# Raw tokens transposed at once, with the norm's weight folded into the low-rank weights

## The chip, the cores and the metric

The kernel runs on one core of a Trainium2 chip. A core has TensorE (PE, which multiplies 128x128 stationary tiles with moving ones into PSUM), VectorE (DVE), ScalarE (ACT), GpSimd (POOL) and SyncE (SP, which here only issues DMAs). The metric is the device time of one execution in microseconds, as the median of several.

## The reference

One decoder layer on x of 512 tokens by 1024 channels, all in float32. What matters here is its start:

```python
h = rms_norm(x, norm_g[l])      # x * rsqrt(mean(x*x) + EPS) * norm_g
proj = h @ w_in[l]
hq, hf, hi, hz, cq, ckv, kr, mz, glog = jnp.split(proj, pts, axis=-1)
y_a = hgrn2_branch(hq, hf, hi, hz, lower_bounds[l], hg_norm_g[l])
y_b = mla_branch(cq, ckv, kr, mz, q_a_g[l], w_uq[l], kv_a_g[l], w_ukv[l])
```

The low-rank columns cq, ckv and kr (384, 256 and 64 wide, 704 together) go through a norm or a rotation of their own. All other columns of proj read the same h. A gated recurrence (y_a), attention (y_b), gates, two projections, the output product and a last norm follow.

## The kernel before

Products are made in three parts: each operand is split into a high part (fp32r) and a low part (the rest), and `mm3` (L99) issues high x high, high x low and low x high into one PSUM bank. The high part is a ScalarE copy, the low part a VectorE subtraction (`load_w`, L110, for weights). The split, transposed input h is `hT`, two tiles of 128 x 8 x 512 (channels of a block k, blocks, tokens).

The first stage (L292 to L347) is written out by hand for PE, ACT and DVE: inside `manual_schedule` each engine runs what the code issues, in that order. Behind it a scheduler chooses the order. Tokens are in four tiles of 128 (t = 0 to 3), channels in eight blocks (k). The stage does, per token tile:

- the root: `squares` (L256) sums the squares on ScalarE and makes the power -0.5 on GpSimd (`power`, L174); tile 0 has its own version with a square root on ScalarE and seven small VectorE instructions (L307 to L317);
- `scaled` (L261): VectorE multiplies x by the root and by norm_g, which four matmuls have spread over the partitions into the two banks `ng` (L302 to L304);
- `turned` (L266): TensorE transposes eight 128x128 blocks, ScalarE copies them as the high part and VectorE subtracts for the low part;
- `c_product` (L277): the first 256 low-rank columns, 24 matmuls a tile, into two banks `c_ps`, with weights split by `c_hi` and `c_lo`.

`idle_mm` (L244) issues matmuls on zeros as filler. Then two banks are copied to `c_sb` (L393), and the second low-rank product makes the other 448 columns (L395 to L400): four tiles of tokens by eight blocks by three parts, 96 matmuls, with four weight pieces of two blocks each (`load_c2`, L287). The first two pieces are split inside the first stage, the other two behind it. PSUM has three `mm` banks: two hold the first product, so the second product's tile 1 waits until the first of them is copied out. The small work on the recurrence's lower bound (`lbw`, L376 to L390) lies between. Behind the 96 matmuls come the recurrence's projections, which read hT and split weights of their own (L129, L130), and the norm, transposes and splits of the low-rank columns (L401 to L429). DMAs are issued by SP in the order of the code; a weight buffer's next load waits for VectorE's low part of the last one.

Of the kernel before, what the change touches and what calls it, by code (L numbers as in the profile page):

```python
# [38 lines left out]
def hybrid_layer(ctx: ExitStack, tc: tile.TileContext, a):  # L39
# [158 lines left out]
    ng_row = st.tile([2, 512], F32, "ng_row")
    ng_r = [st.tile([P, 512], F32R, f"ng_r{i}") for i in range(2)]
    zf = st.tile([P, 512], F32, "zf")  # L200
    nc.gpsimd.memset(zf[:], 0.0)
    nc.gpsimd.memset(pick[:], 0.0)
    nc.gpsimd.memset(pick[0:2, 1], 1.0)
    nc.gpsimd.memset(pick[0:1, 1], 0.0)
    nc.gpsimd.memset(pick[0:1, 0], 1.0)
# [43 lines left out]
    def c_hi(kh, i, eng):  # L249
        eng(c_hl[kh][0][:, half[i]], c_raw[kh][:, half[i]])  # L250

    def c_lo(kh, i, eng):
        hi, lo = c_hl[kh]
        eng.tensor_tensor(lo[:, half[i]], c_raw[kh][:, half[i]], hi[:, half[i]].bitcast(F32), op=ALU.subtract)

    def squares(t):  # L256
        sq = st.tile([P, D], F32, "sq", bufs=2)
        nc.scalar.activation(sq[:], x_sb[t][:], AF.Square, accum_out=rss[t][:, 0:1])
        power(rss[t][:, 0:1], rss[t][:, 0:1], 1.0 / D, EPS, neg_half[:, 0:1])

    def scaled(t):  # L261
        for n in range(2):
            nc.vector.scalar_tensor_tensor(xns[t][:, half[n]], x_sb[t][:, half[n]], rss[t][:, 0:1], ng[n][:],
                                           op0=ALU.mult, op1=ALU.mult)

    def turned(t, k4):  # L266

        ps = ax_tile()
        for k in range(4):
            kk = 4 * k4 + k  # L270
            nc.tensor.transpose(ps[:, k * P : k * P + P], xns[t][:, kk * P : kk * P + P], ident[:])
# [1 line left out]
        nc.scalar.copy(hT[0][sl], ps[:].rearrange("p (k t) -> p k t", k=4))
        return lambda: nc.vector.tensor_tensor(hT[1][sl], ps[:].rearrange("p (k t) -> p k t", k=4),
                                               hT[0][sl].bitcast(F32), op=ALU.subtract)

    def c_product(t, kh, kind, ks=range(4)):  # L277

        l, r = ((0, 0), (0, 1), (1, 0))[kind]
        ps = c_ps[t // 2][:, t % 2 * 256 : t % 2 * 256 + 256]  # L280
        for k in ks:
            nc.tensor.matmul(ps, hT[l][:, 4 * kh + k, t * P : t * P + P], c_hl[kh][r][:, k * 256 : k * 256 + 256],  # L282
                             start=kh == 0 and kind == 0 and k == 0, stop=kh == 1 and kind == FIN and k == 3)
# [1024 lines left out]
```

## Time and profile before

| | us |
|---|---|
| median of 3 runs (606.27 to 607.28) | 607.03 |
| the profiled execution | 606.53 |
| its span on the core | 604.7 |
| granted TensorE clock, mean | 0.996 |
| TensorE busy | 595.2 |
| VectorE / ScalarE / GpSimd busy | 445.2 / 283.0 / 148.3 |

The profiled execution's own time is 1.8 above its span. A row of the order in time reads: start, length, engine, line, operation, what it writes and reads, shape, count; in brackets the engine's idle time before it and what ended that. PE rows are matmuls; they are pipelined, so a row's length is longer than the distance to the next. Line numbers are those of the kernel before unless said otherwise.

### The profile page before, as it was taken

What the parts mean: (1) busy time and instruction counts of PE and PEld (TensorE: products, weight loads), DVE (VectorE), ACT (ScalarE), POOL (GpSimd) and SP (SyncE); (2) the same over time, 40 slices, a digit from 0 to 9 for tenths busy, and PEclk for the clock granted to TensorE, in tenths of its full rate; (3) what the DMA queues carried; (4) which work ended last, traced back from release to release, by engine and by line L of the source; (5) the groups of instructions that cost most, each with busy time, mean ns of one, the idle gap of its engine ahead of it and who ended that gap; (6) DMA issues with size and microseconds to landing.
All of it is one profiled execution on the core that took longest, in us unless ns stands there. A gap on an engine that the chain in (4) does not pass through costs nothing.

```text
span 604.7 us, 8828 instructions
## 1 busy us (share of the span) xinstructions
PE 595.2 (98%) x3198; PEld 501.5 (83%) x3198; DVE 445.2 (74%) x689; ACT 283.0 (47%) x517; POOL 148.3 (25%) x253
## 2 busy tenths in 40 slices
PE   9999999999999999999999999999999999999994
PEld 6998888888888888888888888888888888888883
DVE  7717989599764548959767776778878878466795
ACT  7555245333313342436545554456557764153553
POOL 3107322254350237415245540400000000000003
PEclk9999999999999999999999999999999999999998
DMA  8449479997969967582369676888666656366313
GB/s 281 159 137 345 155 220 370 318 223 169 239 152 253 232 194 155 112 186 76 62 153 175 147 159 154 222 289 244 192 187 204 204 182 188 123 233 257 102 36 139
DMA packets 73036, 115.34 MB, mean 191 GB/s; under 512 B 7561, under 2 KB 37663, under 8 KB 72993
## 3 DMA queue, kind: packets, MB, share of 16 engines
q1 hardware_dynamic: 63740, 90.99, 47.2%
q0 software_dynamic: 8336, 22.55, 20.2%
q10 hardware_dynamic: 916, 1.25, 0.6%
q8 instruction: 25, 0.41, 0.3%
q14 instruction: 19, 0.15, 0.1%
HBM read 106.38 MB, written 39.85 MB: 242 GB/s over the span
## 4 chain that ended last, share of the span: by engine, by line
PE 89%; DVE 4%; DMA 3%; ACT 2%; issue 1%; POOL 1%; SPq 0%; POOLq 0%; ACTq 0%; DVEq 0%
PE mm_ps L102 19%; PE mm_ps L104 19%; PE mm_ps L103 19%; PE ax_ps L889 16%; PE mm_ps L889 3%; PE ax_ps L754 1%; PE ax_ps L728 1%; DMA x<-x 1%; PE mm_ps L282 1%; PE ax_ps L556 1%; DVE ya L1173 1%; PE ax_ps L558 1%; PE ax_ps L518 1%; PE ax_ps L104 1%; PE ax_ps L103 1%
## 5 line engine op out<-in xcount | busy, mean ns | idle before, releaser
L130 DVE TENSOR_TENSOR w_lo<-w_raw,w_hi 128x1024 fp32r<-128x1024 f32 (+3 forms) x116 | 138.9, 1204 | 68.9 <-ACT w_hi L129 66.1
L129 ACT CAST w_hi<-w_raw 128x1024 fp32r<-128x1024 f32 (+3 forms) x116 | 114.8, 1007 | 132.6 <-PE mm_ps L103 54.7
L102 PE MATMUL mm_ps<-hT,w_hi 128*128 128x512 f32 x256 | 101.0, 395 | 0.0
L103 PE MATMUL mm_ps<-hT,w_hi 128*128 128x512 f32 x256 | 100.3, 392 | 0.0
L104 PE MATMUL mm_ps<-hT,w_lo 128*128 128x512 f32 x256 | 100.2, 393 | 0.0
L102 PE MATMUL mm_ps<-w_hi,hT 128*128 128x512 f32 (+1 forms) x160 | 61.7, 390 | 0.0
L103 PE MATMUL mm_ps<-w_lo,hT 128*128 128x512 f32 (+1 forms) x160 | 61.5, 385 | 0.0
L104 PE MATMUL mm_ps<-w_hi,hT 128*128 128x512 f32 (+1 forms) x160 | 61.4, 385 | 0.0
L104 PEld LDWEIGHTS mm_ps<-hT,w_lo 128*128 128x128 f32 x256 | 48.1, 188 | 9.9
L102 PEld LDWEIGHTS mm_ps<-hT,w_hi 128*128 128x128 f32 x256 | 48.1, 188 | 9.5
L103 PEld LDWEIGHTS mm_ps<-hT,w_hi 128*128 128x128 f32 x256 | 48.1, 188 | 9.4
L889 PE MATMUL ax_ps<-w_hi,s 128*128 128x512 f32 x208 | 51.5, 389 | 0.0
L889 PEld LDWEIGHTS ax_ps<-w_hi,s 128*128 128x128 f32 x208 | 39.0, 188 | 8.1
L1190 POOL TENSOR_SCALAR ssum<-ssum 128x1 f32<-128x1 f32 x3 | 0.7, 225 | 163.7 <-ACT z L1177 163.6
L104 PEld LDWEIGHTS mm_ps<-w_hi,hT 128*128 128x128 f32 x160 | 30.1, 188 | 5.5
L102 PEld LDWEIGHTS mm_ps<-w_hi,hT 128*128 128x128 f32 x160 | 30.0, 188 | 5.2
L103 PEld LDWEIGHTS mm_ps<-w_lo,hT 128*128 128x128 f32 x160 | 30.1, 188 | 5.1
L736 ACT ACTIVATE p<-ax_ps,sm 128x128 f32<-128x128 f32 (+3 forms) x32 | 16.8, 526 | 35.6 <-DVE sm L735 35.4
L738 POOL TENSOR_SCALAR p<-p,sm 128x128 f32<-128x128 f32 (+3 forms) x28 | 15.6, 563 | 65.0 <-DVE sm L737 54.3
L889 PE MATMUL ax_ps<-w_lo,s 128*128 128x512 f32 x104 | 27.8, 389 | 0.0
L466 DVE RECIPROCAL tf<-pr 128x512 f32<-128x512 f32 x8 | 26.8, 3348 | 0.1
L889 PEld LDWEIGHTS ax_ps<-w_lo,s 128*128 128x128 f32 x104 | 19.5, 188 | 4.0
(319 smaller groups left out, 1189.1 us busy)
## 6 DMA issues: line engine op xcount, KB each, us to landing
w_raw<-w_in SPq DMA_DIRECT2D x54, 512.0 KB, 7.0
g_t<-w_in SPq DMA_DIRECT2D x16, 512.0 KB, 8.9
w_raw<-g_t SPq DMA_DIRECT2D x16, 512.0 KB, 4.7
g_t<-w_in POOLq DMA_DIRECT2D x8, 512.0 KB, 10.5
pa_t<-w_proj_a SPq DMA_DIRECT2D x8, 512.0 KB, 8.4
g_t<-g_t POOLq DMA_DIRECT2D x8, 512.0 KB, 10.0
out_t<-w_out SPq DMA_DIRECT2D x8, 512.0 KB, 9.6
s<-h POOLq DMA_DIRECT2D x8, 512.0 KB, 11.7
```

Of the source, the lines that this page charges most:

```text
L102: nc.tensor.matmul(ps, lh[lsl], rh[rsl], start=start, stop=False)
L103: nc.tensor.matmul(ps, lh[lsl], rl[rsl], start=False, stop=False)
L104: nc.tensor.matmul(ps, ll[lsl], rh[rsl], start=False, stop=stop)
L129: last_hi[0] = nc.scalar.copy(hi[:, :o], raw[:, :o])
L130: last_lo[0] = nc.vector.tensor_tensor(lo[:, :o], raw[:, :o], hi[:, :o].bitcast(F32), op=ALU.subtract)
L282: nc.tensor.matmul(ps, hT[l][:, 4 * kh + k, t * P : t * P + P], c_hl[kh][r][:, k * 256 : k * 256 + 256], start=kh == 0 and kind == 0 and k ...
L466: nc.vector.reciprocal(rp[:], pr[:])
L518: nc.tensor.matmul(sps[:, sl], kt_[:, sl], v_sb[i][:, (h % 4) * P : (h % 4) * P + P], start=True, stop=True)
L556: nc.tensor.matmul(ops[:, sl], asb[:, sl], v_sb[i][:, (h % 4) * P : (h % 4) * P + P], start=True, stop=i == 0)
L736: last_act[0] = nc.scalar.activation(p[:, :n], sps[:, :n], AF.Exp, scale=SCALE, bias=sm[:, 1:2], accum_out=sm[:, 2:3])
L738: scaled_p = (nc.vector if final else nc.gpsimd).tensor_scalar(p[:, :n], p[:, :n], sm[:, 3:4], 0.5, op0=ALU.mult, op1=ALU.mult)
L889: nc.tensor.matmul(ps[:, o : o + n], ap[i][:, k, t * P : t * P + P], w[k // 2][j][:, k % 2, o : o + n], start=fresh and c == 0, stop=c == ...
```

## The change

- x is transposed as it is loaded, before any norm: `turned` reads `x_sb` and fills `xT`, a new pair like hT. A third copy, plain, goes to `ya` (the recurrence's later output buffer, allocated earlier).
- norm_g is loaded as eight rows, transposed once into the column tile `gcol`, and multiplied into the low-rank weights as they are split: `times_g` makes the high part on ScalarE with a scale, and the low part on VectorE with one three-operand instruction, a block at a time (256 or 448 wide).
- The tokens' roots `rs` (all four by `squares`, which now needs no special version) are applied where the low-rank banks are copied to `c_sb`, as a scale of the ScalarE copy.
- h itself is made later: VectorE makes four diagonal tiles of roots, four matmuls with ones spread them over the partitions (`scales`), VectorE multiplies ya by norm_g and the roots (eight instructions of 128x512), and ScalarE and VectorE split the result into hT (eight each).
- ident and the norm's rows are loaded from ScalarE's queue, ident no longer from SP's. The warm-up activation is Tanh, not Sqrt.

```diff
     load_x(0, 2)
-    nc.scalar.dma_start(ng_row[:], a["norm_g"].rearrange("l (n c) -> (l n) c", n=2))
-    nc.sync.dma_start(ident[:], a["c_ident"])
+    nc.scalar.dma_start(ident[:], a["c_ident"])
+    nc.scalar.dma_start(g_rows[:], a["norm_g"].rearrange("l (k p) -> (l k) p", p=P))
...
+    def times_g(hi, lo, src, k0, n, width):
+
+        for k in range(n):
+            sl, g = slice(k * width, k * width + width), gcol[:, k0 + k : k0 + k + 1]
+            nc.scalar.activation(hi[:, sl], src[:, sl], AF.Copy, scale=g)
+            nc.vector.scalar_tensor_tensor(lo[:, sl], src[:, sl], g, hi[:, sl].bitcast(F32), op0=ALU.mult, op1=ALU.subtract)
...
-            nc.tensor.transpose(ps[:, k * P : k * P + P], xns[t][:, kk * P : kk * P + P], ident[:])
+            nc.tensor.transpose(ps[:, k * P : k * P + P], x_sb[t][:, kk * P : kk * P + P], ident[:])
...
+        nc.scalar.copy(xT[0][sl], v)
+        nc.vector.tensor_tensor(xT[1][sl], v, xT[0][sl].bitcast(F32), op=ALU.subtract)
+        return lambda: nc.scalar.copy(ya[sl], v)
...
     with tc.manual_schedule(engines={mybir.EngineType.PE, mybir.EngineType.Activation, mybir.EngineType.DVE}):
         nc.vector.memset(zero[:], 0.0)
+        nc.scalar.activation(warm[:], eps, AF.Tanh)
+        idle_mm(5)
+        plain = [turned(0, 0), turned(0, 1)]
+        ps = ax_tile()
+        nc.tensor.transpose(ps[:, :KD], g_rows[:], ident[:KD, :KD])
+        nc.vector.tensor_copy(gcol[:], ps[:, :KD])
+        for f in plain:
+            f()
+        idle_mm(6)
+        c_split(0)
+        c_product(0, 0, 0)
+        c_product(0, 0, 2)
+        plain = [turned(1, 0), turned(1, 1)]
+        c_product(0, 0, 1)
+        c_split(1)
+        c_products(1, 0)
+        c_products(0, 1)
...
+        c_products(2, 0)
+        plain = [turned(3, 0), turned(3, 1)]
+        c_products(2, 1)
+        c_second = [load_c2(j) for j in range(2)]
+        for f in plain:
+            f()
         for t in range(1, NT):
+            squares(t)
+        c_products(3, 0)
+        c_products(3, 1)
...
-    for t2, ps in enumerate(c_ps):
-        nc.scalar.copy(c_sb[:, 2 * t2 : 2 * t2 + 2, 0:256], ps[:].rearrange("p (t c) -> p t c", t=2))
+    for t in range(NT):
+        nc.scalar.activation(c_sb[:, t, 0:256], c_ps[t // 2][:, t % 2 * 256 : t % 2 * 256 + 256], AF.Copy, scale=rs[:, t : t + 1])
     c_second += [load_c2(j) for j in range(2, 4)]
+    scales = ax_tile()
+    for t in range(NT):
+        nc.vector.tensor_scalar(diag[t][:], ident[:], rs[:, t : t + 1], None, op0=ALU.mult)
+        nc.tensor.matmul(scales[:, t * P : t * P + P], ones[:], diag[t][:], start=True, stop=True)
+    for k in range(KD):
+        nc.vector.scalar_tensor_tensor(ya[:, k], ya[:, k], gcol[:, k : k + 1], scales[:], op0=ALU.mult, op1=ALU.mult)
+        split(hT[0][:, k], hT[1][:, k], ya[:, k])
```

The next pieces show the order that each engine now runs; line numbers in them are each kernel's own. First TensorE inside the second low-rank product, before: mm_ps_438, 464 and 490 are the banks of token tiles 0, 1 and 2, w_hi_427 and w_lo_428 the third weight piece (blocks k 4 and 5). 29 of the 96 matmuls stand ahead of the first row on w_hi_427, 35 ahead of the first on w_lo_428.

```order
L102 MATMUL mm_ps_490<-w_hi_361,hT0_125 128x448
L103 MATMUL mm_ps_490<-w_lo_362,hT0_125 128x448
L102 MATMUL mm_ps_438<-w_hi_427,hT0_125 128x448
L102 MATMUL mm_ps_464<-w_hi_427,hT0_125 128x448
L104 MATMUL mm_ps_490<-w_hi_361,hT1_126 128x448
L102 MATMUL mm_ps_490<-w_hi_367,hT0_125 128x448
L103 MATMUL mm_ps_490<-w_lo_368,hT0_125 128x448
L104 MATMUL mm_ps_490<-w_hi_367,hT1_126 128x448
L103 MATMUL mm_ps_438<-w_lo_428,hT0_125 128x448
```

The same place in the changed kernel: mm_ps_462 and 488 are the banks of tiles 0 and 1, w_hi_414 and w_lo_415 the third weight piece, and diag0 to diag3 the four tiles of roots. Twelve matmuls of tile 0 (k 0 to 3) stand ahead of these rows.

```order
L370 MATMUL ax_ps_429<-diag0_104,ones_103 128x128
L370 MATMUL ax_ps_429<-diag1_105,ones_103 128x128
L102 MATMUL mm_ps_488<-w_hi_328,xT0_126 128x448
L103 MATMUL mm_ps_488<-w_lo_329,xT0_126 128x448
L104 MATMUL mm_ps_488<-w_hi_328,xT1_127 128x448
L102 MATMUL mm_ps_488<-w_hi_328,xT0_126 128x448
L370 MATMUL ax_ps_429<-diag2_106,ones_103 128x128
L370 MATMUL ax_ps_429<-diag3_107,ones_103 128x128
L103 MATMUL mm_ps_488<-w_lo_329,xT0_126 128x448
L104 MATMUL mm_ps_488<-w_hi_328,xT1_127 128x448
L102 MATMUL mm_ps_462<-w_hi_414,xT0_126 128x448
L102 MATMUL mm_ps_488<-w_hi_336,xT0_126 128x448
```

The next row is the first on w_lo_415. So the third weight piece is now read behind 18 of the 96 matmuls (its low part behind 20), not 29 (35), and the four matmuls on the roots stand ahead of it.

ScalarE from tile 3's high parts on, before: hT is the high part, w_hi 128x896 a weight piece of the second product, c_sb the copies of the banks.

```order
L273 CAST hT_125<-ax_ps 128x4x128 x4
L129 CAST w_hi<-w_raw 128x896 x2
L393 COPY c_sb<-mm_ps 128x2x256 x2
L129 CAST w_hi<-w_raw 128x896
L379 ACT_TABLE_LOAD
L379 ACTIVATE lbw<-lbw 128x16
L129 CAST w_hi<-w_raw 128x896
L400 COPY c_sb<-mm_ps 128x448
```

And in the changed kernel, from the same place: the third and fourth weight pieces are the second group of w_hi.

```order
L264 CAST xT_126<-ax_ps 128x4x128 x2
L248 ACTIVATE w_hi<-w_raw,gcol 128x448 x4
L266 COPY ya<-ax_ps 128x4x128 x2
L253 ACTIVATE sq,rs<-x 128x1024 x3
L365 ACTIVATE c_sb<-mm_ps,rs 128x256 x4
L351 ACTIVATE lbw<-lbw 128x16
L248 ACTIVATE w_hi<-w_raw,gcol 128x448 x4
L171 CAST hT_128<-ya 128x512 x4
```

The two plain copies and the squares of three token tiles now stand between the first two weight pieces and the copies of the banks; a table load is gone.

VectorE behind the first stage in the changed kernel: diag_107 is diag3, and w_lo 128x448 x4 are the low parts of the third and fourth piece.

```order
L369 TENSOR_SCALAR diag_107<-ident,rs 128x128
L340 TENSOR_SCALAR hg_half<-par 128x1
L348 TENSOR_TENSOR lbw<-par 128x8
L349 TENSOR_TENSOR lbw<-par,lbw 128x8
L350 TENSOR_TENSOR lbw<-par,lbw 128x8
L352 TENSOR_TENSOR lbw<-lbw 128x8
L353 RECIPROCAL lbw<-lbw 128x8
L355 TENSOR_TENSOR lb<-lbw 128x8
L360 TENSOR_SCALAR c_403<-lb 128x8
L361 TENSOR_SCALAR c1n<-lb 128x8
L362 TENSOR_SCALAR c_405<-lb 128x8
L249 SCALAR_TENSOR_TENSOR w_lo<-w_raw,gcol,w_hi 128x448 x4
```

Before, the third piece's low part stood ahead of the second half of lbw; now all of lbw, and diag3 ahead of it, come first. L352 waits for ScalarE's exponential (L351). Behind these rows stand the eight multiplications of ya, the eight low parts of hT, and then the recurrence's first weights.

More of the change, by code (lines that the diff above doesn't have):

```diff
@@ L186, in hybrid_layer @@
     maskf = cw.tile([P, 2, P], F32, "maskf")
+    rs = cw.tile([P, NT], F32, "rs")
+    gcol = cw.tile([P, KD], F32, "gcol")
+    ones = cw.tile([P, P], F32, "ones")
+    diag = [cw.tile([P, P], F32, f"diag{t}") for t in range(NT)]
     st = Pool("start", "right")
+    raw_pool = Pool("raw_tokens", "left")
     ident = const.tile([P, P], F32, name="ident")
@@ L192, in hybrid_layer @@
     nc.gpsimd.memset(neg_half, -0.5)
+    nc.gpsimd.memset(ones[:], 1.0)
     zero = st.tile([P, 512], BF16, "zero")
-    pick = st.tile([P, 2, P], F32, "pick")
-    pick_r = st.tile([P, 2, P], F32R, "pick_r")
     warm = st.tile([P, 1], F32, "warm")
[L198 to L205, printed above, removed]
+    g_rows = st.tile([KD, P], F32, "g_rows")
     x_sb = [st.tile([P, D], F32, "x", bufs=NT) for _ in range(NT)]
+    xT = [raw_pool.tile([P, KD, S], F32R, f"xT{i}") for i in range(2)]
     hT = [hpool.tile([P, KD, S], F32R, f"hT{i}") for i in range(2)]
+    ya = ypool.tile([P, H, S], F32, tag="ya", name="ya")
     w_c0 = w_in[:, COL_C : COL_C + 256].rearrange("(k p) c -> p k c", p=P)
@@ L247, in idle_mm @@
             nc.tensor.matmul(idle[:], zero[:, :P], zero[:], start=True, stop=True)
[L249 to L254, printed above, removed]
-    def squares(t):
[L257 to L264, printed above, removed]
+    def times_g(hi, lo, src, k0, n, width):
[3 more added lines that the diff above has]
+            nc.vector.scalar_tensor_tensor(lo[:, sl], src[:, sl], g, hi[:, sl].bitcast(F32), op0=ALU.mult, op1=ALU.subtract)
+    def squares(t):
+        sq = st.tile([P, D], F32, "sq")
+        nc.scalar.activation(sq[:], x_sb[t][:], AF.Square, accum_out=rs[:, t : t + 1])
+        power(rs[:, t : t + 1], rs[:, t : t + 1], 1.0 / D, EPS, neg_half[:, 0:1])
     def turned(t, k4):
@@ L302, in hybrid_layer @@
-        for x in range(2):
-            for n in range(2):
-                nc.tensor.matmul(ng[n][:], pick_r[:, n], ng_r[x][:], start=x == 0, stop=x == 1)
-            idle_mm(2 + 2 * x)
-        sq, rs = st.tile([P, D], F32, "sq", bufs=2), rss[0]
-        v, y, e = [st.tile([P, 1], F32, f"rsq{i}") for i in range(3)]
-        for n in range(2):
-            nc.scalar.activation(sq[:, half[n]], x_sb[0][:, half[n]], AF.Square, accum_out=rs[:, n : n + 1])
-        nc.vector.tensor_scalar(v[:], rs[:, 0:1], 1.0 / D, EPS, op0=ALU.mult, op1=ALU.add)
@@ L312, in hybrid_layer @@
-        nc.scalar.activation(y[:], rs[:, 1:2], AF.Sqrt, scale=1.0 / D, bias=v[:])
-        nc.vector.tensor_scalar(e[:], rs[:, 1:2], 1.0 / D, v[:], op0=ALU.mult, op1=ALU.add)
-        nc.vector.tensor_scalar(e[:], e[:], -0.5, None, op0=ALU.mult)
-        nc.vector.reciprocal(y[:], y[:])
-        nc.vector.tensor_scalar(v[:], y[:], y[:], e[:], op0=ALU.mult, op1=ALU.mult)
-        nc.vector.tensor_scalar(rs[:, 0:1], v[:], 1.5, y[:], op0=ALU.add, op1=ALU.mult)
-        scaled(0)
-        for i in range(2):
-            c_hi(0, i, nc.scalar.copy)
@@ new lines, in hybrid_layer @@
+        c_products(1, 0)
+        c_products(0, 1)
+        for f in plain:
+            f()
+        plain = [turned(2, 0), turned(2, 1)]
+        c_products(1, 1)
+        squares(0)
+        for f in plain:
+            f()
+        c_products(2, 0)
+        plain = [turned(3, 0), turned(3, 1)]
+        c_products(2, 1)
+        c_second = [load_c2(j) for j in range(2)]
+        for f in plain:
+            f()
+        for t in range(1, NT):
+            squares(t)
+        c_products(3, 0)
@@ L430, in hybrid_layer @@
     cw.close()
-    ya = ypool.tile([P, H, S], F32, tag="ya", name="ya")
     ma_pool = Pool("mla_a", "right")
```

74 lines of the change are left out of this document (19 added, 55 removed).

## The prediction

> **What bounds the kernel now.** I read the page first, then busy time by stretch, then the order in time of the first 45 us, which is all that the change touches. The page:
>
> ```profile
> span 604.7 us, 8828 instructions
> PE 595.2 (98%) x3198; PEld 501.5 (83%) x3198; DVE 445.2 (74%) x689; ACT 283.0 (47%) x517; POOL 148.3 (25%) x253
> PE 89%; DVE 4%; DMA 3%; ACT 2%; issue 1%; POOL 1%; SPq 0%; POOLq 0%; ACTq 0%; DVEq 0%
> ```
>
> TensorE is busy for 98% of the span and holds 89% of the chain that ended last. By stretch (busy us of each engine, with instruction counts):
>
> ```profile
> core 0: us, PE busy (x) PEld busy (x) DVE busy (x) ACT busy (x) POOL busy (x), PEclk, DMA share, GB/s
> 0.00:15.00 15.00, 13.79 (x72) 9.07 (x73) 11.02 (x24) 10.63 (x21) 5.26 (x16) 1.00 0.82 281
> 15.00:25.00 10.00, 9.72 (x81) 9.18 (x79) 7.37 (x12) 4.58 (x9) 2.30 (x7) 1.00 0.30 89
> 25.00:45.00 20.00, 20.00 (x100) 18.50 (x100) 6.21 (x16) 11.55 (x24) 0.00 (x0) 1.00 0.54 179
> 70.00:550.00 480.00, 480.00 (x2608) 405.06 (x2607) 357.82 (x551) 221.19 (x404) 121.24 (x195) 1.00 0.73 196
> ```
>
> TensorE has no hole from 25 us on: 20.00 of 20, later 480.00 of 480. The work behind the low-rank stage is the same in both kernels, so the difference in time is the difference in one moment: when the first matmul on hT behind the low-rank products starts. These TensorE rows (start, length, both in us) carry that moment and the prices of the stage:
>
> ```profile
> 1.18 3.17 PE L247 MATMUL ax_ps<-zero 128*128 128x512 bf16 x7 [1.18 <-DVE zero L293]
> ...
> 6.43 1.04 PE L247 MATMUL ax_ps<-zero 128*128 128x512 bf16 x4
> ...
> 8.76 0.74 PE L282 MATMUL mm_ps<-w_hi,hT 128*128 128x256 f32 x4
> ...
> 19.53 1.03 PE L271 MATMUL ax_ps<-ident,xn 128*128 128x128 f32 x8
> ...
> 22.79 1.60 PE L282 MATMUL mm_ps<-w_hi,hT 128*128 128x256 f32 x12
> ...
> 24.80 0.23 PE L364 MATMUL ax_ps<-ident,rows 22*128 22x22 f32 x1
> ...
> 24.96 0.47 PE L102 MATMUL mm_ps<-w_hi,hT 128*128 128x448 f32 x1
> ...
> 44.52 0.39 PE L102 MATMUL mm_ps<-hT,w_hi 128*128 128x512 f32 x1
> ```
>
> The first low-rank product ends at 24.8, the second (96 matmuls, 24.96 to 44.52, 0.203 us each) runs without a wait, and the moment is 44.52. A transpose takes 0.109 (eight in 1.03, the last one's length of 0.27 taken off), a 256-wide matmul 0.12 (twelve in 1.60, less 0.28). A 512-wide one takes 0.42 before about 6 us and 0.22 after (7 in 3.17, 4 in 1.04): TensorE starts at half speed.
>
> **The change: its start.** The two halves of token tile 0 and the first low-rank weights land as these ScalarE rows show:
>
> ```profile
> 4.33 0.63 ACT L310 ACTIVATE sq<-x 128x512 f32<-128x512 f32 x1 [0.25 <-DMA x<-x]
> ...
> 7.09 1.14 ACT L250 CAST w_hi<-w_raw 128x512 fp32r<-128x512 f32 x2 [1.71 <-DMA w_raw<-w_in]
> ```
>
> So the second half is there at 4.3, the weights at 7.1 at the latest (they are now issued one place earlier; I take no gain from that). Removed are the broadcast of norm_g (four matmuls, the idle ones among them, the copies and the split ahead), tile 0's root, and eight scalings xn on VectorE, which made each tile's transposes wait for its root. The transposes now wait for x and ident alone. Prices (ScalarE groups, mean ns of one, and rows in time):
>
> ```profile
> L273 ACT CAST hT<-ax_ps 128x512 fp32r<-128x512 f32 x8 | 4.5, 587 | 4.4 <-PE ax_ps L271 4.3
> L258 ACT ACTIVATE sq<-x 128x1024 f32<-128x1024 f32 x3 | 3.2, 1068 | 0.0
> L423 ACT ACTIVATE cT<-ax_ps,par 128x512 fp32r<-128x512 f32 x5 | 3.0, 689 | 1.1 <-PE ax_ps L422 1.1
> L405 ACT ACTIVATE csq<-c_sb 128x256 f32<-128x256 f32 x4 | 1.6, 402 | 0.0
> ```
>
> ```profile
> 9.09 1.07 ACT L258 ACTIVATE sq<-x 128x1024 f32<-128x1024 f32 x1
> ...
> 10.05 0.20 ACT L258 ACTIVATION_READ_ACCUMULATOR sq<-x 128x1 f32 x1
> ...
> 20.16 1.08 ACT L273 CAST hT<-ax_ps 128x512 fp32r<-128x512 f32 x2 [2.71 <-PE ax_ps L271]
> ...
> 20.78 1.29 DVE L274 TENSOR_TENSOR hT<-ax_ps,hT 128x512 fp32r<-128x512 f32 x2 [1.29 <-ACT hT L273]
> 21.12 1.79 ACT L129 CAST w_hi<-w_raw 128x896 fp32r<-128x896 f32 x2
> ```
>
> Second half's transposes at half speed: 4.4 + 4 x 0.22 + 0.2 = 5.5. Cast 0.59, VectorE's low part 0.69 (two in 1.29): 6.8. The plain copy to ya waits for that and holds ScalarE until 7.3. The norm weight's column (g_rows transposed, copied) is ready by 6.9. Now the weights' high parts, 256 wide with a scale from SBUF: the trace has none. Without a scale 402 ns; a scale adds 689 - 587 = 102 ns; ends 0.40 and 0.60 (double the surcharge), I take 0.50, one every 0.40 since neighbours overlap by 0.1. The first product's four matmuls start at 7.85, the last at 9.05 (before: 8.76).
>
> From 9.2 TensorE has no reason to wait: 56 matmuls x 0.12 and 24 transposes x 0.109, with 0.4 for two waits on PSUM buffers, are 9.75 us to the end of tile 3's transposes (18.95, results at 19.1), and 36 x 0.12 + 0.16 (L364) more put the start of the second product at **23.4, against 24.96: 1.55 us won**. I checked each cast and each low part against this line; the closest, tile 1's low part, arrives just in time.
>
> **The change: what waits then.** ScalarE now also makes eight plain copies, and in its program the roots' squares of tiles 1 to 3 stand behind tile 3's copies, and the last four scaled weight pieces (k 4 to 7 of the second product) behind those. From 19.1: tile 3's second cast 0.5 (two in 1.08), four scaled casts 448 wide at 0.56 (896 wide take 0.84 each in the row above, so 448 take 0.47, and 0.1 for the scale) = 2.24, two plain copies 1.0, three squares at 1.19 (9.09 to 10.25, and a turn of 0.03) = 3.57: **26.4**. Behind the last square:
>
> ```profile
> 10.34 0.19 POOL L176 TENSOR_SCALAR rs<-rs 128x1 f32<-128x1 f32 x1 [7.80 <-ACT sq L258]
> ...
> 10.62 0.56 POOL L177 TENSOR_TENSOR rs<-rs,fixed 128x1 f32<-128x1 f32 x1
> ...
> 11.21 1.41 DVE L263 SCALAR_TENSOR_TENSOR xn<-x,rs,ax_ps 128x512 f32<-128x512 f32 x2 [0.97 <-POOL rs L177]
> ...
> 12.53 0.69 DVE L254 TENSOR_TENSOR w_lo<-w_raw,w_hi 128x512 fp32r<-128x512 f32 x1
> 12.53 0.74 POOL L176 TENSOR_SCALAR rs<-rs 128x1 f32<-128x1 f32 x1
> ...
> 25.28 0.15 DVE L368 TENSOR_SCALAR hg_half<-par 128x1 f32<-128x1 f32 x1
> ...
> 25.63 0.16 DVE L378 TENSOR_TENSOR lbw<-par,lbw 128x8 f32<-128x8 f32 x1
> ...
> 27.64 0.22 ACT L379 ACTIVATE lbw<-lbw 128x16 f32<-128x16 f32 x1
> ...
> 27.89 0.17 DVE L380 TENSOR_TENSOR lbw<-lbw 128x8 f32<-128x8 f32 x1 [0.44 <-ACT lbw L379]
> 28.09 0.20 DVE L381 RECIPROCAL lbw<-lbw 128x8 f32<-128x8 f32 x1
> ...
> 29.92 0.17 DVE L388 TENSOR_SCALAR c<-lb 128x8 f32<-128x8 f32 x1
> ```
>
> Root on GpSimd, 10.25 to 11.21: 0.96. Then, in VectorE's order, diag3 (0.2), hg_half and lbw (25.28 to 25.79: 0.5), the exponential on ScalarE with its handovers (0.3), and the rest of lbw and c (0.4 from 27.89 to 28.29, 0.2 for L383, 0.33 for the three of L388: 0.95), and only then the low part of k 4 (448 wide; a 512-wide three-operand one takes 0.74: 0.65, and 0.05 to TensorE). Together 3.6: **30.0**. TensorE has reached that matmul by about 29: from 23.4 it runs 12 matmuls to 25.85, waits for the copies that free the first product's bank (behind the squares, about 27.1), does six more, with the four on diag between, and then stands before the low part of k 4. Behind it follow 76 of the 96: 76 x 0.203 = 15.4. The moment is **45.4 instead of 44.52: +0.9 us**. The four diag matmuls (0.11 as a transpose, 0.47 as the longest row above) lie in the wait and cost nothing here; if the wait were gone they would cost 0.4 to 1.9, I take 0.7.
>
> A row tells what GpSimd can add: a root's first step took 0.74 beside VectorE's 0.69 on two SBUF inputs at 12.53, and 0.19 at 10.34 alone. [...] In the new order VectorE has finished such work (22.6) before the first of the three roots (24): no cost; beside it, 0.55 more.
>
> hT comes in time. VectorE ends the low parts at 31.9; eight scalings (0.70 each, two in 1.41) and eight low parts (0.64) last until 42.6, and the next weights' low part (below) until 43.8, needed at 46.3. What covers it is VectorE's idle 12.16:
>
> ```profile
> 42.40 3.50 DVE L130 TENSOR_TENSOR w_lo<-w_raw,w_hi 128x1024 fp32r<-128x1024 f32 x3 [12.16 <-ACT w_hi L129]
> ```
>
> The table load that goes (Tanh is warmed up instead of Sqrt) stood before L379 and is in the sum by its absence. The sum against the profiled execution: 606.5 + 0.9 = 607.4. That execution lies 0.5 under the median of 607.03, so on the median's footing the forecast is **607.9**, no change that a measurement can tell (0.2%, 1.2 us), with a lean to slower. Its own range is 0.5 either way.
>
> **Rivals.**
> - *The gain is carried through.* If ScalarE's chain is over a us before TensorE needs it, the moment is 23.4 + 19.5 + 0.7 = 43.6: 0.9 less, 606.1; with a start half a us earlier 605.6. For it: ScalarE was idle at 47% on the page; against it: its program order. It decides if k 4's low part is there by 28.3.
> - *The start is late.* ident and g_rows now go through ScalarE's queue, beside tile 0's halves. If ident lands at 4.9 and not by 4.3, everything moves by 0.6: 608.5. Bounds: 3.3 to 7.1, where its neighbours landed; I take 4.
> - *Half speed lasts longer.* Slower: before, the rate doubles near 6 us with TensorE busy since 1.18; now it waits for tile 0 between. If the doubling came at 9.5, transposes, the four matmuls of the first low part and the filler cost 0.9 + 0.5 + 0.2 more: 609.5. [...]
> - *hT is late.* VectorE's 16 new instructions would have to be a quarter dearer than their rows (2.5 us of cover); beyond that every us counts: 608.9 at 3.5 over.
>
> **Numbers.** Forecast 0.55, gain carried 0.18, late start 0.14, half speed 0.08, hT late 0.05. The range runs from the second case's 606.1 to just under the half-speed one's: 609.3. Faster by over 0.2% (under 605.8): a little over half of the gain case, 0.10. Slower: a fifth of the forecast, most of the late start, all of half speed and half of the last, 0.33. The rest, 0.57, is within.
>
> **What would show it.** Second product's first matmul near 23.4; a wait of about 0.9 us before the sixth group of its rows and another before the first low part of k 4 at 30.0, put down to ScalarE's copy and VectorE's low part; the first matmul on hT at 45.4 without a wait on hT. Wrong if the second product has no hole, if it starts after 24, or if hT is waited for.

## The result, and the profile after

| | before | after |
|---|---|---|
| median, us (lowest to highest, runs) | 607.01 (606.27 to 607.44, 6) | 612.97 (612.07 to 614.90, 6) |
| the profiled execution | 606.53 | 612.07 |
| its span | 604.7 | 610.0 |

The changed kernel is slower: its time is 1.0105 times that of the kernel before (this is the ratio in what follows), with a 95% interval of 1.0091 to 1.0119. That is 6.0 us by the medians and 5.5 between the two profiled executions; the changed kernel's is the fastest of its six. The page of the changed kernel (busy time, and the chain that ended last):

```profile
span 610.0 us, 8841 instructions
PE 597.3 (98%) x3197; PEld 502.5 (82%) x3197; DVE 449.9 (74%) x700; ACT 291.9 (48%) x539; POOL 145.1 (24%) x250
PE 81%; DVE 7%; issue 5%; POOL 3%; ACT 3%; DMA 1%; SPq 0%; POOLq 0%; DVEq 0%; ACTq 0%
```

TensorE's share of the chain fell from 89% to 81%. The stretches that the prediction looked at, in the changed kernel:

```profile
0.00:15.00 15.00, 13.15 (x66) 8.72 (x67) 6.28 (x14) 8.97 (x18) 0.46 (x7) 1.00 0.83 281
15.00:25.00 10.00, 10.00 (x83) 9.78 (x82) 5.43 (x11) 8.79 (x17) 0.99 (x4) 1.00 0.38 118
25.00:45.00 20.00, 19.12 (x97) 16.99 (x96) 15.66 (x35) 16.94 (x39) 1.98 (x5) 1.00 0.52 162
70.00:550.00 480.00, 477.40 (x2585) 402.18 (x2585) 356.66 (x548) 220.82 (x404) 122.68 (x198) 1.00 0.72 194
```

The 20.00 of 25 to 45 became 19.12, which was forecast. The 480.00 of 70 to 550 became 477.40, which was not. TensorE's row of the moment, and the waits of TensorE over the whole span (total, times, longest):

```profile
24.06 0.47 PE L102 MATMUL mm_ps<-w_hi,xT 128*128 128x448 f32 x1
...
45.99 0.39 PE L102 MATMUL mm_ps<-hT,w_hi 128*128 128x512 f32 x1
```

```profile
PE mm_ps L104 <- DVE w_lo L130: 2.6, 1, 2.6
PE ax_ps L242 <- DVE zero L295: 1.2, 1, 1.2
PE ax_ps L261 <- DMA ident<-c_ident: 0.6, 1, 0.6
PE mm_ps L102 <- ACT c_sb L365: 0.5, 1, 0.5
PE mm_ps L103 <- DVE w_lo L249: 0.3, 1, 0.3
```

The moment is 45.99, 1.47 later than before. Far behind the stage comes the longest wait, 2.60 for a low part of weights; such a time in which TensorE stands is called a hole below. TensorE's rows around it:

```profile
82.46 0.39 PE L103 MATMUL mm_ps<-hT,w_hi 128*128 128x512 f32 x1
85.45 0.50 PE L104 MATMUL mm_ps<-hT,w_lo 128*128 128x512 f32 x1 [2.60 <-DVE w_lo L130]
...
87.49 0.63 PE L104 MATMUL mm_ps<-hT,w_lo 128*128 128x512 f32 x1
87.92 0.63 PE L102 MATMUL mm_ps<-hT,w_hi 128*128 128x512 f32 x1
...
90.36 0.39 PE L102 MATMUL mm_ps<-hT,w_hi 128*128 128x512 f32 x1
90.59 0.39 PE L103 MATMUL mm_ps<-hT,w_hi 128*128 128x512 f32 x1
```

```profile
87.00:88.00 1.00, 1.00 (x4) 0.74 (x3) 1.00 (x2) 0.00 (x0) 0.00 (x0) 0.50 0.87 257
```

Behind the hole the matmuls start 0.43 apart from 86.6 to 89.6 and not 0.23: the granted clock of that window is 0.50. The sum is closed by a group that both kernels have, the first scores of the recurrence, in the order in time of before and of after:

```profile
103.94 1.15 PE L532 MATMUL ax_ps<-qi,ki 128*64 128x64 f32 x32
```

```profile
109.90 1.15 PE L511 MATMUL ax_ps<-qi,ki 128*64 128x64 f32 x32
```

They start 5.96 later: 1.47 of the first stage, 2.60 of the hole, and 1.89 of half speed and of the restart around it. From there to 400 us the distance stays at 5.92. So the loss has two places, and the larger one lies behind everything that the diff touches.

**Why VectorE was late at 82.9.** The awaited low part belongs to the first query weights of the first pair of heads. VectorE runs in the order that the scheduler chose, and that order is not the same in the two kernels, although the code behind the stage is. VectorE's rows, before and after (qr, qs, qh, p are whole sums of hT that later block products need, "early sums"; pr is the scan of the second head's forget gate, which needs GpSimd's fr; kpe a low part read from PSUM):

```profile
77.57 0.68 DVE L483 TENSOR_TENSOR ki<-k,tf 128x512 f32<-128x512 f32 x1
78.17 0.68 DVE L777 SCALAR_TENSOR_TENSOR p<-p,qr 128x512 f32<-128x512 f32 x1
78.78 0.68 DVE L820 TENSOR_TENSOR qh<-hT,hT 128x512 f32<-128x512 f32 x1
79.38 1.21 DVE L130 TENSOR_TENSOR w_lo<-w_raw,w_hi 128x1024 fp32r<-128x1024 f32 x1
80.52 0.68 DVE L820 TENSOR_TENSOR qs<-hT,hT 128x512 f32<-128x512 f32 x1
```

```profile
71.04 0.68 DVE L172 TENSOR_TENSOR kpe<-ax_ps,kpe 128x512 fp32r<-128x512 f32 x1
73.42 1.23 DVE L444 TENSOR_TENSOR_SCAN pr<-f,fr 128x512 f32<-128x512 f32 x1 [1.69 <-POOL fr L441]
...
81.35 0.69 DVE L463 TENSOR_TENSOR ko<-ki,pr 128x512 f32<-128x512 f32 x1
81.95 0.68 DVE L756 SCALAR_TENSOR_TENSOR p<-p,qr 128x512 f32<-128x512 f32 x1
82.55 1.11 DVE L799 TENSOR_TENSOR qh<-hT,hT 128x512 f32<-128x512 f32 x1
83.59 0.68 DVE L799 TENSOR_TENSOR qs<-hT,hT 128x512 f32<-128x512 f32 x1
84.19 1.21 DVE L130 TENSOR_TENSOR w_lo<-w_raw,w_hi 128x1024 fp32r<-128x1024 f32 x1
```

The low part now has ko and qs ahead of it too, and VectorE stood for 1.69 before the scan. Its rows leave no other gap between 66 and 92. Before, the low part ended at 80.59 and TensorE's first matmul on it started at 80.65, so there was next to no room. After, TensorE comes to it 2.20 later (82.85), but the low part ends 4.81 later (85.40). VectorE's rows behind the stage are the same in both kernels, if in another order, until 65.13 before and 66.97 after, 1.84 apart; from there to the low part only ko and qs are more (0.60 each), and the wait of 1.69 is almost all of the rest.

GpSimd's rows, before and after (L463 and L442 are the same instruction, k of the second head):

```profile
66.03 2.25 POOL L463 TENSOR_SCALAR k<-tf,c1n,c 128x512 f32<-128x512 f32 x1 [6.85 <-ACT tf L460]
```

```profile
66.75 4.86 POOL L442 TENSOR_SCALAR k<-tf,c1n,c 128x512 f32<-128x512 f32 x1 [6.60 <-ACT tf L439]
71.56 0.79 POOL L415 DMA_DIRECT2D qtab<-c_qtab  x1
72.38 0.64 POOL L464 TENSOR_TENSOR k<-ko,gh 128x256 f32<-128x256 f32 x1
73.11 0.28 POOL L441 TENSOR_SCALAR fr<-f 128x16 f32<-128x16 f32 x1
```

The same instruction took 2.25 before and 4.86 after. In both it ended soon (0.74 and 0.57) behind the start of kpe. kpe started at 67.54 before, ahead of ko, f and k (L465); after, it started at 71.04, behind all three.

### The profile page after: what moved, and what is told of

It reads as the page before. It is cut to its first block, busy times and chain, and to the rows that moved or that the text cites. A ratio compares the mean times of both kernels' runs of the same rounds, so it can differ in the third digit from the quotient of the medians.

```text
span 610.0 us, 8841 instructions
## 1 busy us (share of the span) xinstructions
PE 597.3 (98%) x3197; PEld 502.5 (82%) x3197; DVE 449.9 (74%) x700; ACT 291.9 (48%) x539; POOL 145.1 (24%) x250
## 3 DMA queue, kind: packets, MB, share of 16 engines
q1 hardware_dynamic: 63596, 90.92, 46.5%
## 4 chain that ended last, share of the span: by engine, by line
PE 81%; DVE 7%; issue 5%; POOL 3%; ACT 3%; DMA 1%; SPq 0%; POOLq 0%; DVEq 0%; ACTq 0%
PE ax_ps L868 17%; PE mm_ps L104 16%; PE mm_ps L102 16%; PE mm_ps L103 16%; PE mm_ps L868 3%; PE ax_ps L733 1%; PE mm_ps L273 1%; PE ax_ps L707 1%; PE ax_ps L535 1%; DVE tf L445 1%; DMA w_raw<-w_in 1%; DVE ya L1152 1%; PE ax_ps L537 1%; PE ax_ps L497 1%; PE ax_ps L104 1%
## 5 line engine op out<-in xcount | busy, mean ns | idle before, releaser
L130 DVE TENSOR_TENSOR w_lo<-w_raw,w_hi 128x1024 fp32r<-128x1024 f32 (+2 forms) x112 | 135.3, 1213 | 61.9 <-ACT w_hi L129 53.3
L129 ACT CAST w_hi<-w_raw 128x1024 fp32r<-128x1024 f32 (+2 forms) x112 | 111.2, 1008 | 133.4 <-PE mm_ps L103 57.1
L102 PE MATMUL mm_ps<-w_hi,hT 128*128 128x512 f32 x128 | 50.3, 396 | 0.0
L103 PE MATMUL mm_ps<-w_lo,hT 128*128 128x512 f32 x128 | 49.8, 391 | 0.0
L104 PE MATMUL mm_ps<-w_hi,hT 128*128 128x512 f32 x128 | 49.7, 390 | 0.0
L104 PEld LDWEIGHTS mm_ps<-w_hi,hT 128*128 128x128 f32 x128 | 24.0, 188 | 5.1
L102 PEld LDWEIGHTS mm_ps<-w_hi,hT 128*128 128x128 f32 x128 | 24.0, 188 | 4.8
L103 PEld LDWEIGHTS mm_ps<-w_lo,hT 128*128 128x128 f32 x128 | 24.1, 188 | 4.7
```

The costliest lines, as they stand in the source:

```text
L102: nc.tensor.matmul(ps, lh[lsl], rh[rsl], start=start, stop=False)
L103: nc.tensor.matmul(ps, lh[lsl], rl[rsl], start=False, stop=False)
L104: nc.tensor.matmul(ps, ll[lsl], rh[rsl], start=False, stop=stop)
L129: last_hi[0] = nc.scalar.copy(hi[:, :o], raw[:, :o])
L130: last_lo[0] = nc.vector.tensor_tensor(lo[:, :o], raw[:, :o], hi[:, :o].bitcast(F32), op=ALU.subtract)
```

## The experiments

The theory: the loss is 1.47 of the first stage (three squares in a row at the end of ScalarE's program, and a first product that starts late), and 4.5 of a hole that comes from the order in which the scheduler queues VectorE's work behind the stage. The rivals: the stage or the late norm makes it all; or the hole comes because the stage ends late. Times below are medians; the kernel before took 606.5 to 606.7 beside all of them. "The stage ended at" gives the start of the first matmul on hT behind the low-rank products, 44.52 before and 45.99 after. `issue_after` adds an edge: on that instruction's engine, what the block issues stays behind it.

**1. The low part ahead of two sums.** `los` lists all low parts of weights as they are issued; `first` is its length ahead of the first pair's query product.

```diff
+        if not pair:
+            q_lo[0] = los[first]
...
-            early_sums(kh[1])
+            with tc.issue_after(q_lo[0].ins):
+                early_sums(kh[1])
```

> Changed kernel with one edge: on VectorE the first low part of the first query weights goes ahead of the two whole sums qs and qh of the second early sums; TensorE's order is as in the changed kernel. Theory (a hole behind the low-rank stage, made by VectorE's order): those two took 1.11 and 0.68 (starts 82.55 and 83.59, the low part 84.19), so the low part ends near 83.8 and not 85.4; TensorE's hole of 2.60 at 82.85 shrinks to about 1.0; if the half speed behind it (nine matmuls at 0.43 and not 0.23, 1.8) goes too, 612.07 falls to about 608.7, if it stays, to about 610.4. Rival (the loss is made in the first stage or the late norm): nothing moves ahead of the low-rank stage's end, 612 to 613.

Measured: 611.56 (610.88 to 612.21), ratio 1.0084 (1.0069 to 1.0099). The hole is still 2.0, and the half speed with it (granted clock 0.50 from 88 to 89). The two sums did move behind the low part, but VectorE had lost as much earlier, waiting for a weight's high part:

```profile
55.43 1.23 DVE L132 TENSOR_TENSOR w_lo<-w_raw,w_hi 128x1024 fp32r<-128x1024 f32 x1 [1.44 <-ACT w_hi L131]
```

In the changed kernel's profiled execution that wait was not there. The run doesn't decide; it shows that VectorE's whole queue from 50 to 85 is one chain, into which a load that lands a microsecond late goes in full. That may also be a reason for the wide scatter of the changed kernel's runs (2.8 us, before 1.2), but no run here shows that.

**2. kpe ahead of the first early sums.**

```diff
+    kpe_lo = nc.vector.tensor_tensor(kpe[1], ps[:], kpe[0].bitcast(F32), op=ALU.subtract)
...
-            early_sums(kh[0])
+            with tc.issue_after(kpe_lo.ins):
+                early_sums(kh[0])
```

> Changed kernel with one edge: on VectorE the low part kpe (reads PSUM) goes ahead of the four early sums (two SBUF inputs each) and not behind them. Theory (GpSimd's k of the second head, L442, is held while VectorE runs the sums and is let in by the first instruction that reads PSUM: it began 66.75, ended 71.61, 0.57 behind kpe's start at 71.04): k ends near 69, the scan no longer waits for fr (1.69 idle on VectorE at 73.4 goes), the low part of the query weights ends about 1.7 earlier, near 83.7, and TensorE's hole is about 0.9; 608.5 to 610.5. Rival (k is slow by itself or waits for something else): k still takes about 4.9, hole 2.6, 612 to 613.

Measured: 610.19 (609.81 to 611.85), ratio 1.0066 (1.0051 to 1.0081). GpSimd's row for the same k:

```profile
66.85 2.46 POOL L443 TENSOR_SCALAR k<-tf,c1n,c 128x512 f32<-128x512 f32 x1 [6.59 <-ACT tf L440]
...
70.07 2.23 POOL L465 TENSOR_TENSOR k<-ko,gh 128x256 f32<-128x256 f32 x1
```

4.86 became 2.46, ending 0.58 behind the start of kpe (68.73). The next GpSimd instruction then took 2.23, beside the early sums, for 0.64 in the changed kernel, so VectorE still waited 0.88 for fr. The hole is 1.83, without half speed behind it (granted clock 1.00 from 83 to 89). The order did shorten k; the gain was half of what I expected.

**3 and 4. All early sums of the first pair behind the low part,** in the changed kernel (3) and in the kernel before (4); the call moves behind the query product:

```diff
-        else:
-            early_sums(kh[0])
...
+        if not pair:
+            with tc.issue_after(los[first].ins):
+                early_sums(kh[0])
```

> Changed kernel with all early sums of the first pair put behind the first low part of the query weights on VectorE (the planner then moves some 60 rows of TensorE too). Theory: no hole near 82.85 and no half speed behind it, 2.60 and 1.8 less: 612.07 falls to about 607.7, still above the kernel before by the 1.47 by which the low-rank stage ends later. Rival (first stage makes the loss): 612 to 613. If another wait takes its place: 609 to 611.

> Kernel before with the same edit as in the changed kernel with its early sums behind the low part. Theory: the kernel before has no hole there, so nothing is to be won: 606.5 to 607.5. Rival (the early sums cost TensorE time in any order): faster by 1 or more.

Measured: (3) 608.96 (608.49 to 610.34), ratio 1.0045 (1.0030 to 1.0060); no hole near 83, although the stage ended at 46.21, but one of 2.48 at 127.8, on the recurrence's k. (4) 609.59 (609.27 to 609.88), ratio 1.0052 (1.0036 to 1.0069): slower by 3.0, with holes of 0.77, 0.18 and 0.95 between 123.8 and 135.8. In that execution the stage ended at 45.25, 0.73 late, for weights that landed late (7.81), so not all of the 3.0 need be the order's. Both times fell outside what I expected, but the hole near 83 did go. The sums are not free wherever they stand: VectorE has so little room from 60 to 130 that work put off in one place is missing in another. For the cause this helps in two ways: in the changed kernel another order leaves no hole near 83 behind an equally late stage, and the kernel before becomes some 3 us slower by an edit of the order alone.

**5. Both edges,** those of 1 and 2 together.

> Changed kernel with both edges: kpe ahead of the first early sums, and the low part of the query weights ahead of qs and qh of the second. Theory (VectorE's chain ends last): with kpe alone that low part ran 83.48 to 84.69 with qh (1.11, from 81.84) and qs (0.68) ahead of it, so now it runs 81.84 to 83.05 and the hole, 1.83 at 84.75 with kpe alone, falls to 0.2 or less; what is left is the 1.47 of the front, 607.5 to 608.5 for 606.6 of the kernel before. Rival (the hole has another cause, such as a load that lands late): a hole of 1 or more stays, 609.5 or more.

Measured: 609.81 (607.68 to 611.23), ratio 1.0049 (1.0031 to 1.0067). In the profiled execution (610.37) holes of 1.18 at 84.5 and 0.77 at 100 are left; the stage ended at 46.45 there. The lowest run is where I expected all. So edges mend the order in part. VectorE stood 0.40 for a weight's high part at 55.1 here; that a late load or a late stage opens the hole again is how I read it, not shown.

**6. Seven idle matmuls at the start,** which cover the wait for the identity.

```diff
-        idle_mm(5)
+        idle_mm(7)
```

> Changed kernel with seven idle matmuls at the start and not five, so that TensorE doesn't stand between 3.49 and 4.07; all orders else as in the changed kernel. Theory (the 0.58 of idling kept the half speed on until 7.8): the transposes of tile 0 end up to 0.4 earlier, the first product starts near 8.0 to 8.2 and not 8.47, the first matmul on the whitened tokens near 45.6 and not 46.0. Rival (the chain of ScalarE and VectorE sets the first product, not the clock): first product within 0.1 of 8.47. The hole behind stays.

Measured, one run: 614.06. The first product started at 8.48, as in the changed kernel and as the rival has it. But the half speed wasn't shortened enough to matter: the transposes ended at 6.05, in the changed kernel at 6.04. Experiment 2, whose front is the changed kernel's, tells more. Full speed came at 4.7 there and the transposes ended at 5.38, yet the first product started at 8.50. ScalarE waited for the weights until 7.94, and TensorE for ScalarE's casts:

```profile
PE mm_ps L273 <- ACT w_hi L248: 1.6, 1, 1.6
```

So the clock didn't set the first product in experiment 2, the weights did.

In the run with seven idle matmuls the stage nevertheless ended at 45.33, 0.66 earlier: the scheduler had put other matmuls ahead of k 4's low part, and the wait of 0.34 for it was gone. And the hole was the largest of all:

```profile
PE mm_ps L104 <- DVE w_lo L130: 3.2, 1, 3.2
```

An earlier end of the stage didn't shrink the hole. But VectorE also stood 1.39 for a weight's high part at 54.8, as it did for 1.44 in experiment 1, so this run alone doesn't speak against lateness as the cause.

**7. Squares early.** ScalarE has holes in the first stage; each tile's squares go into one: tile 0's ahead of the first `c_product`, tile 1's ahead of tile 2's transposes, tile 2's behind tile 2's plain copies, tile 3's behind the casts of `load_c2`.

```diff
+        squares(0)
...
+        squares(1)
...
+        squares(2)
...
+        squares(3)
-        for t in range(1, NT):
-            squares(t)
```

> Changed kernel with each tile's squares put into the holes of ScalarE's program (one tile each, the last ahead of the last two plain copies) and not three in a row at its end. Theory, front: the waits of 0.53 at 27.7 and 0.35 at 30.5 go, the first matmul on the whitened tokens comes at about 45.1 and not 46.0. Theory, behind: the planner then orders VectorE another way, the first low part of the query weights stands ahead of six instructions that were ahead of it (some 4 us), so no hole near 83: 607 to 607.8, still 0.5 to 1 above the kernel before. Rival (the hole is set by the time at which the stage ends, not by the order): a hole of about 2 stays, 609 to 611.

Measured: 608.20 (606.94 to 610.67), ratio 1.0030 (1.0013 to 1.0047). ScalarE's end of the stage, in the changed kernel and here:

```profile
26.77 0.18 ACT L253 ACTIVATION_READ_ACCUMULATOR sq<-x 128x1 f32 x1
26.86 1.55 ACT L365 ACTIVATE c_sb<-mm_ps,rs 128x256 f32<-128x256 f32 x4
```

```profile
24.31 1.59 ACT L366 ACTIVATE c_sb<-mm_ps,rs 128x256 f32<-128x256 f32 x4
...
112.19 0.62 ACT L171 CAST qn<-p 128x512 fp32r<-128x512 f32 x1 [6.84 <-DMA h<-qn]
```

The copies out of the bank start 2.55 earlier, both waits are gone, and the stage ends at 44.55, level with the kernel before (44.52). VectorE's order behind it is another one, and the hole at 83 is gone, as the theory had it. The median lies above its range because of a new hole, which begins with the last row: qn's tile is written again only when the store of its old content has landed, ScalarE waits for that until 112.19, VectorE's masked copies are queued behind, and TensorE waits 1.86 for them at 114.8. In the kernel before the same wait cost VectorE 2.98 at 109.9 and TensorE nothing.

**8. The whole front tuned** (7, with the seven idle matmuls, the norm weight's transposes first, and the scaled casts ahead of the plain copies).

> Changed kernel with seven idle matmuls, the norm weight's columns ahead of the tokens' transposes, the scaled casts ahead of the plain copies, and the squares early. Theory: scaled casts start near 7.1 (when the weights have landed) and not 7.90, the first product near 7.7 and not 8.47, both waits behind the squares gone: the first matmul on the whitened tokens at 44.2 to 44.6, as in the kernel before (44.52), and no hole near 83: 606.2 to 607.2 against 606.6. Rival (the columns of the norm weight land late and hold the transposes): the first product no earlier than 8.4, 607 to 608.

Measured: 608.52 (606.70 to 612.03), ratio 1.0039 (1.0016 to 1.0062). The first product started at 8.49, no earlier. What held it, in ScalarE's rows:

```profile
7.93 1.31 ACT L248 ACTIVATE w_hi<-w_raw,gcol 128x256 fp32r<-128x256 f32 x3 [1.42 <-DMA w_raw<-w_in]
```

ScalarE was free from 6.5 on; the first weights landed at 7.9 (7.1 in the kernel before). The start is the rival's, its cause is not: the column of the norm weight was transposed at 4.33. The stage ended at 45.35, not at 44.2 to 44.6. The hole at 116.9 was 2.99 in this execution, with half speed behind it (granted clock 0.50 from 119 to 121).

**9. The kernel before, made late.**

```diff
             lo = nxt
+        idle_mm(7)
     tc.no_sync_barrier()
```

> Kernel before with seven more idle matmuls of TensorE (0.216 each, 1.5) right ahead of the second low-rank product, every other instruction in its old order: the low-rank stage then ends as late as in the changed kernel (about 46.0 for 44.52). Theory (the hole behind the stage comes from the order in which VectorE's work is queued, not from the late end): no hole near 83, all moves by 1.5: 608.1 for 606.7. Rival (a stage that ends late makes the hole): a hole of 1 to 3 and 610 to 612.

Measured: 607.90 (607.29 to 608.84), ratio 1.0025 (1.0015 to 1.0034), 1.4 over the 606.46 beside it. TensorE's waits, all of them:

```profile
PE ax_ps L247 <- DVE zero L293: 1.2, 1, 1.2
PE ax_ps L271 <- DVE xn L263: 0.2, 1, 0.2
```

A stage that ends 1.3 later (45.81) makes no hole as long as the order behind it is the old one. The recurrence's first scores come 1.30 later too (105.24 for 103.94), and the median is up by 1.4: the delay passes on to the end, as the prediction had it.

**10. The tuned front, ident on SP's queue again, and qn's last cast and low part held behind the masked copies and the head's squares.**

```diff
-    nc.scalar.dma_start(ident[:], a["c_ident"])
+    nc.sync.dma_start(ident[:], a["c_ident"])
...
+            with tc.issue_after(last_asb[0].ins), tc.issue_after(last_osq[0].ins):
+                keep(4, "qn", e12)
```

> The changed kernel with the tuned front (seven idle matmuls, norm weight first, scaled casts first, squares early), the identity back on SP's queue behind the first tokens, and the last cast and low part of the second early sums (qn, which wait for a store to land) put behind the masked copies and the head's squares. Theory, front: with one queue the first weights land near 7.1 to 7.4 and not 7.9, the first product starts at 7.7 to 7.9, the stage ends at 44.3 to 44.9. Theory, behind: no hole near 83 and none near 115 (2.99 at 116.93 without these two edges): 606.2 to 607.0 for 606.7. Rival (DMA landings and not the queue set the first weights; another wait follows): 607.5 to 609.

Measured: 606.74 (605.55 to 609.47), ratio 1.0006 (0.9994 to 1.0018). The front did not come as expected: the first weights landed at 8.9, later than with two queues, the first product started at 9.45 and the stage ended at 46.20. That is as late as in the changed kernel, and yet there is no hole behind the stage at all in this execution (607.48): the order is another. One queue for the identity didn't bring the weights earlier. With the front of the kernel before alone, they were there between 6.72 (experiment 9) and 7.81 (experiment 4), so the landing itself scatters by a microsecond.

**11. The kernel before with qn held.** The edges of 10 (behind the masked copies and squares) alone.

> Kernel before with qn's last cast and low part put behind the masked copies and the head's squares. In the kernel before VectorE stood 2.98 at 109.9 on that wait, but TensorE had other work: no change, 606.3 to 607.1. Rival (the wait costs TensorE something later): faster by 0.5 or more.

Measured: 606.68 (606.05 to 608.00), ratio 1.0004 (0.9995 to 1.0013): no change, as expected.

**12. The changed front with all edges behind it,** those of 1, 2 and 11.

> The changed kernel, front as it is, with all edges behind the stage: kpe ahead of the first early sums, the low part of the query weights ahead of qs and qh, and qn behind the masked copies. Theory: only the 1.47 of the front and what a late weight load adds are left: 608.0 to 609.0 for 606.7 (609.8 without the last edge, with holes of 1.18 and 0.77). Rival (another place becomes late): 609.5 to 611.

Measured: 610.06 (609.58 to 610.40), ratio 1.0059 (1.0046 to 1.0073). A hole of 1.75 at 85.2 again, with VectorE 1.52 late for a weight's high part at 55.8. My expectation fell: edges alone don't bring VectorE's chain in time.

**13. The kernel before with its low part late,** nothing else:

```diff
-        pq = proj_ch(w_in, COL_Q + cc, hT)
+        if pair:
+            pq = proj_ch(w_in, COL_Q + cc, hT)
+        else:
+            with tc.issue_after(last_k[0].ins):
+                pq = proj_ch(w_in, COL_Q + cc, hT)
```

> Kernel before with its front untouched and one edge behind the stage: the low parts of the first query weights go behind the second head's k on VectorE, that is behind six instructions more (some 4 us: ends near 84.7 and not 80.59; TensorE needs it about 81.2). Theory (order alone makes the hole): TensorE stands 1 to 3.5 there, with half speed behind it if it stands over 2: 608.5 to 612 for 606.5. Rival (only a late stage or the changed memory makes a hole): 606 to 607.

Measured: 608.10 (607.83 to 609.81), ratio 1.0026 (1.0014 to 1.0037). TensorE stood here:

```profile
83.60 0.52 PE L510 MATMUL ax_ps<-ident,k 128*128 128x128 f32 x3 [1.33 <-DVE k L487]
```

Order alone makes a hole in the kernel before. The hole is at the low end of what I expected, and the time just below it: the scheduler filled the place with other matmuls, so TensorE's wait is put down to k, one row ahead of the low part.

**14. Just two things in the changed kernel:** squares early (7) and qn held (11).

> The changed kernel with just two things: squares early, and qn's last cast and low part behind the masked copies and the head's squares; idle matmuls, identity and column order as in the changed kernel. Theory (front waits and holes behind are the whole loss): the stage ends near 44.6 as with the squares early alone, no hole near 83 or 115: 606.2 to 607.0 for 606.5, no difference from the kernel before. Rival (something else is left, such as the late norm's work on VectorE): 607.5 or more.

Measured: 606.53 (605.72 to 607.34), ratio 0.9994 (0.9984 to 1.0004). The stage ended at 44.79, and of the hole this is left:

```profile
PE mm_ps L104 <- DVE w_lo L131: 0.4, 1, 0.4
```

The whole loss is taken up by two edits that change only the order of the work. The late norm, the scaled casts and the eight plain copies then cost nothing and win nothing that a measurement can tell. No version here beats the kernel before. As squares early moves the stage's end and VectorE's order at once, this run doesn't divide the loss between the two places.

## Why the prediction was wrong

- **Right: the mechanism of the stage.** The second product had two waits, on ScalarE's copies (0.53 at 27.7) and on the first low part of k 4 (0.34 before 30.47), and the gain of the early start was given back there. The second wait was shorter than forecast (about 1), because TensorE came to it later. Forecast for the low part 30.0, measured 30.42; ScalarE's last square 26.4, measured 26.95; the root behind it 0.96, measured 0.91; scaled casts 0.50 at a distance of 0.40, measured 0.50 and 0.40; hT's low parts at 42.6, measured 42.29, and hT was not waited for.
- **A term too small: the start.** The first product began at 8.46 and not 7.85, and this 0.6 carried through: the second product started at 24.06 for 23.4, just past the 24 that the prediction named as a sign of being wrong, and the moment was 45.99 for 45.4. Two terms were short. The working let four of tile 0's transposes run before 4.4; the identity landed at 4.03, so all eight ran behind that at half speed (0.21 apart), and the second half's results were there at 6.04 and not 5.5. And it took the weights to be there at 7.1; where ScalarE stood waiting for them in kernels with two queues they came at 7.93 to 8.07 (experiments 2, 5 and 8), which alone gives the same start. The 0.6 is the size of the rival of the late start, but that rival needed the identity at 4.9: the agreement is luck. Over the traces that leave the front alone, the moment lay at 44.5 to 45.3 before (4 traces) and at 45.9 to 46.5 after (6), on average 1.3 apart.
- **Right: half speed costs little there.** With one and the same front it lasted until 4.7 (experiment 2), 7.8 (the changed kernel) and 10.0 (experiments 3 and 12), and the second product started at 24.12, 24.06, 24.27 and 24.21. The rival's price, 1.6 for a doubling at 9.5, was far too high.
- **Wrong: the sentence on which the sum rested,** "The work behind the low-rank stage is the same in both kernels, so the difference in time is the difference in one moment". The work is the same, its order is not. The scheduler put VectorE's work behind the stage into another order; there VectorE had no room, and a low part came 2.6 too late. With half speed behind it that is 4.5 of the 5.96, and it put the time outside the range; with the start's 0.6 alone the forecast would have been 608.5, inside it. The inference from a moment to the end holds where the order is kept (experiment 9); with the order changed it doesn't. No rival of mine lay behind the stage at all.
- **A reading that was wrong.** The 47% that I gave as ScalarE's idle share is its busy share on the page. It was an argument for a rival; the sum didn't use it.
- **What I could have seen.** TensorE without a hole from 70 to 550 says nothing of how near the next engine is. From 60 to 85 alone VectorE is busy for 25.00 of 25 in the kernel before, as full as TensorE:

```profile
60.00:85.00 25.00, 25.00 (x115) 20.60 (x114) 25.00 (x32) 8.96 (x14) 8.44 (x13) 1.00 0.49 160
```

- **Shown and argued.** Shown: order without lateness makes a hole in the kernel before (13), lateness without the new order makes none there (9), another order leaves no hole near 83 in the changed kernel though the stage ends as late (3 and 10), and two edits of the order take up the whole loss (14). Not shown: the very order of the changed kernel was not put into the kernel before. Of the 2.6, VectorE's rows give the division in one execution (ko and qs 1.2 and the wait for GpSimd 1.69, while TensorE itself came later by 0.36 more than the rows ahead of these); experiment 2 confirms 0.8 for GpSimd's k beside the sums, and what a load's landing adds differs from run to run. Why the scheduler chose this order stays open.

## What to carry to other kernels

Where a scheduler orders what lies behind an edit, compare every engine's order behind it, row by row, before calling that work unchanged, and look for a stretch in which a second engine is as full as the bound one: there a move of one or two rows opens a hole. Put reductions that a later scale needs into the holes of their engine's program as the data comes, not in a row at its end. And price a hole of TensorE by more than its length: here 2.60 of standing cost 1.89 more.

## What the runs showed of the hardware

- **GpSimd's k beside a row of VectorE instructions.** A 128x512 instruction with one input tile took 0.88 at 55.1 in the changed kernel, where VectorE ran rows with one SBUF tile and a column of factors as inputs. At 66.75 it took 4.86, beside seven VectorE instructions without a gap, most of them with two SBUF inputs; the same instruction took 2.25 in the kernel before and 2.46 in experiment 2. It ended 0.57 behind the start of kpe, which reads PSUM, in the changed kernel, 0.58 in experiment 2 and 0.74 in the kernel before. What made it long, and whether kpe is what ended it, isn't settled by these runs.
- **Half speed behind a hole.** The granted clock was 0.50 behind holes of 2.60 (the changed kernel, from 86.28 to 89.70, 3.41 us), 2.00 (experiment 1, from 88 to 89, with 0.76 from 89 to 90), 2.99 (experiment 8, from 119 to 121) and 3.2 (experiment 6, from 87 to 91). It was 1.00 around holes of 1.75 (experiment 12, from 84 to 90), 1.83 (experiment 2, from 83 to 89), 1.86 (experiment 7, from 113 to 119) and 2.48 (experiment 3, from 126 to 132). Why 2.00 brought half speed and 2.48 did not is not shown. At the start of the changed kernel the clock's records begin at 7.78; ahead of that the views of stretches give 1.00, although 512-wide idle matmuls start 0.43 apart there and 0.22 apart behind it.
- **The first weights' landing.** Where ScalarE stood waiting for them, they came at 6.72 (experiment 9) to 7.81 (experiment 4) in five executions with the front of the kernel before (7.09 in its own), at 7.93 (experiment 8) to 8.07 in three with the identity on ScalarE's queue, and at 8.9 in experiment 10. Why is not shown.
